# Index scores interleaved pair by pair with the projections of a hybrid attention block on one NeuronCore

## The chip, the core and the metric

One core of one Trainium2 chip runs the whole layer. The metric is device time in microseconds of one execution; the kernel before takes 1416.54 us in the median of three runs (1414.64 to 1420.17). The core's engines run side by side, each through its own queue in order: TensorE (PE, matrix products, with a clock of which a share is granted), VectorE (DVE), ScalarE (ACT), GpSimd (POOL), and SP, which issues the DMAs. Products land in PSUM, from which VectorE and ScalarE read them.

## The reference

A layer with two mixers over the same projected input, then a feed-forward part. What matters here is the first mixer's index scores with their top-k, and the second mixer's decays:

```python
# x: (1, 1024, 1024); h = rms_norm(x); proj = h @ w_in, split into
# q_a, c_kv, q_idx (8 heads of 64), k_idx (64), w_idx (8), q_b, k_b, v_b (4 heads of 128), a_b, b_b, z_b
rel   = relu(einsum('bqhd,bsd->bqhs', qi_b, k_idx))          # per block of 128 rows
score = einsum('bqhs,bqh->bqs', rel, wi_b)
score = where(key_pos < limit, score, -inf)                  # chunk-causal, chunks of 64
_, idx = top_k(score, 256)                                   # the keys that the attention may use
...
g     = cumsum(-exp(a_log) * softplus(a_b + dt_bias))        # in chunks of 64
decay = exp(where(causal, g[..., :, None] - g[..., None, :], -inf))
lower = where(strict, (k * beta) @ k.T * decay, 0);  t_inv = (eye + lower)^-1
...
mix = concat([o_a, o_b]) @ w_out;  x = x + rms_norm(mix)
x = x + rms_norm(square(relu(rms_norm(x) @ w_mlp_in)) @ w_mlp_out)
```

## The kernel before

Products are made in about fp32 precision from split operands: `mm3` (L199 to L201) issues three matmuls, high by high, low by high and high by low. A projection of 128 columns (`project_slowly`) takes eight steps of `mm3` for each half of the 1024 rows, 48 matmuls, into a two-bank accumulator (`psw`, pool of two). The list `plan` gives the order: `kw` (index key, head weights and gates' inputs), four `qi` (two index heads each), four times `kb` and `qb` (a head of k and of q), four `vb`, four `z`, `c`, four `qa`.

What follows a projection depends on its kind. `evac_pair` stores a pair of index heads split into a high and a low part (`QS`, L409 and L410). `conv` (L585 to L590) runs the causal convolution of k, q or v from the accumulator: one ScalarE copy, three VectorE steps over 1024 columns (L587), a ScalarE SiLU. `delta_head` (L679 to L702) turns a head of k and q, sums squares and multiplies the products of k and q with the decays. `base_blocks` (L720 to L722) inverts the small triangles, `post_c` finishes the latents.

`decays(n)` makes the decay matrix of one block of rows: two GpSimd products (L663), two matmuls (L664), an exponential (L666), a select on GpSimd (L667) and a DMA to `e_d`, from which `delta_head` loads. All eight are called behind `kw`. They and the convolutions share a ring of four buffers, `tmp`.

`scores(b)` makes the index scores of one block of 128 queries, chunk by chunk of at most 512 keys: for each of eight heads two matmuls (L480, L481) into one of four banks (`psx`), a ReLU in place on ScalarE (L486), and a multiply-add onto the score in SBUF on VectorE (L487; the first head has one step, L484). All six blocks with a search, 7 down to 2, are called behind the fourth `qi`. Then `pi_close` frees `QS` and `dna` is opened in its place, which holds what `delta_head` needs.

`bisect()` finds the 256th largest score of each row bit by bit, 32 rounds. In a round ScalarE counts three blocks (L521), VectorE three (L527), and VectorE flips the candidate's bit (L530 to L532); the next round needs all of it. Three steps on the least score follow (L548 to L552), and then the masks of the six blocks (L566 to L577). The generator is advanced by the projections: one to three rounds behind each, by the table `rate`, the rest at the end.

`Flow` is a planner that runs while the program is traced. Each part is a generator that yields the time at which it may go on, or the name of an event; the planner takes the first, by rank, that is due, and keeps estimated times of the engines (`use`, with `dve` and `act`). So it fixes the program order, not the executed one: the compiler's scheduler goes through the program in that order as a priority and puts later instructions ahead where an earlier one cannot go. Each engine then executes its queue in order.

When the projections are done, buffers are freed, the event `room` is set, and attention, the delta rule's chain and the output follow.

Of the kernel before, what the change touches and what calls it, by code (L numbers as in the profile page):

```python
# [139 lines left out]
def block_kernel(ctx: ExitStack, tc: tile.TileContext, x, w_in, c_norm, w_uk, w_uv, rel_bias, conv_w, a_log,  # L140
# [148 lines left out]
    warmr = pl.t(px, [P, 1024], F32R, "warmr")  # L289
    V.memset(warmr.bitcast(F32), 0.0)  # L290
    ps = psw()
    for _ in range(10):
        PE.matmul(ps[:, 0:512], warm[:, 0:P], warm, start=True, stop=True)
    ps = psw()
    two = warmr[:, 0:512].rearrange("p (a b) -> p b a", a=2)
    forms = [(warmr[:, 0:P], two), (warmr[:, 0:P], warmr[:, 0:512].rearrange("p (a b) -> p b a", a=4)),
             (warmr[:, 0:256:2], two), (warmr[:, 0:P], warmr[:, 0:256].rearrange("p (a b) -> p b a", a=2))]
    for lhs, rhs in forms:
        o = ps[:, 0:rhs.shape[1] * rhs.shape[2]].rearrange("p (a b) -> p a b", b=rhs.shape[2])
        for _ in range(4):  # L300
            PE.matmul(o, lhs, rhs, start=True, stop=True)
    for _ in range(4):
        for r in range(2):
            rs = slice(64 * r, 64 * r + 64)
            PE.matmul(ps[:, 512 * r:512 * r + 512].rearrange("p (b a) -> p b a", a=2), warmr[rs, 0:P], two[rs],
                      start=True, stop=True)
# [168 lines left out]
    def scores(b):  # L475
        for s0, w in cuts(P * (b + 1)):
            dst = score[:, soff[b] + s0:soff[b] + s0 + w]
            for h in range(8):
                ps = psx()
                PE.matmul(ps[:, :w], QS[:, h, b * P:(b + 1) * P], KH[:, s0:s0 + w], start=True, stop=False)  # L480
                PE.matmul(ps[:, :w], QS[:, h, b * P:(b + 1) * P], KL[:, s0:s0 + w], start=False, stop=True)  # L481
                wh = wab[:, b, h:h + 1]
                if h == 0:
                    V.tensor_scalar(dst, ps[:, :w], 0.0, wh, op0=OP.max, op1=OP.mult)  # L484
                else:
                    S.activation(ps[:, :w], ps[:, :w], AF.Relu)  # L486
                    V.scalar_tensor_tensor(dst, ps[:, :w], wh, dst, op0=OP.mult, op1=OP.add)  # L487
        G.memset(score[0:64, soff[b] + P * b + 64:soff[b] + P * (b + 1)], PAD)
# [461 lines left out]
    def projections():  # L950
        nonlocal dna, dn, dn_close
        for i, (kind, p) in enumerate(plan):
# [19 lines left out]
            if kind == "kw":  # L972
# [3 lines left out]
                for n in range(NB):  # L976
                    decays(n)
# [815 lines left out]
```

## Time and profile before

| | before |
|---|---|
| median of 3 runs | 1416.54 us |
| the profiled execution | 1417.32 us |
| its span, first to last instruction | 1415.6 us |
| mean granted TensorE clock | 0.950 |
| TensorE busy | 1299.8 us, 92% |
| VectorE busy | 1104.6 us, 78% |
| ScalarE busy | 730.1 us, 52% |
| GpSimd busy | 272.0 us, 19% |
| DMA | 211.24 MB, mean 149 GB/s |

Times are from one profiled execution, counted from its first instruction. A share of the span is a mean over stages; the stage that the change touches is the first third, up to about 460 us. "Idle before" is the time that an engine stood ahead of an instruction, and the arrow names what ended it.

### The profile page before, as it was taken

How to read it: one execution, taken by the hardware profiler on the slowest of the kernel's cores; microseconds unless marked ns; L12 is line 12 of the kernel's file. 1: busy time of each engine (PE TensorE's matmuls, PEld its weight loads, DVE VectorE, ACT ScalarE, POOL GpSimd, SP SyncE). 2: the span in 40 equal slices, each digit the busy share in tenths (PEclk: the TensorE clock that was granted, in tenths of full speed). 3: DMA queues.
4: the chain of work that ended last, by engine and by line, in shares of the span. 5: the costliest groups of instructions: out<-in, count | busy, mean ns of one | idle time of the engine just before them, and what ended most of it. 6: DMA issues, size and time to landing. Idle time of an engine off the chain costs nothing. (4 is left out here: it accounts for less than half of the span.)

```text
span 1415.6 us, 20269 instructions
## 1 busy us (share of the span) xinstructions
PE 1299.8 (92%) x6643; PEld 1120.9 (79%) x6643; DVE 1104.6 (78%) x2551; ACT 730.1 (52%) x1521; POOL 272.0 (19%) x296
## 2 busy tenths in 40 slices
PE   7898997998885999999999899999998799999995
PEld 4687894776675899997888688888887688888884
DVE  5524668999999798888768468878876887978975
ACT  5433436777651677677546456566565233333422
POOL 3154221121205335327420000000000000000023
PEclk8899998999995899999999899999999899999998
DMA  6133112456225433333556825555557956645224
GB/s 191 57 85 82 30 46 60 119 157 156 60 72 138 133 95 93 100 116 114 173 163 201 271 101 208 209 208 201 199 200 256 400 173 237 216 141 194 66 79 169
DMA packets 182931, 211.24 MB, mean 149 GB/s; under 512 B 28001, under 2 KB 123434, under 8 KB 182698
## 3 DMA queue, kind: packets, MB, share of 16 engines
q1 hardware_dynamic: 182826, 209.94, 46.3%
q8 instruction: 53, 0.87, 0.3%
q14 instruction: 52, 0.43, 0.1%
HBM read 136.48 MB, written 74.99 MB: 149 GB/s over the span
## 5 line engine op out<-in xcount | busy, mean ns | idle before, releaser
L199 PE MATMUL two<-hTH,wh 128*128 128x512 f32 (+1 forms) x416 | 166.8, 403 | 26.8 <-ACT tmp L424 16.0
L200 PE MATMUL two<-hTL,wh 128*128 128x512 f32 (+1 forms) x416 | 167.0, 401 | 0.0
L201 PE MATMUL two<-hTH,wl 128*128 128x512 f32 (+1 forms) x416 | 165.6, 398 | 0.0
L1750 POOL TENSOR_TENSOR tmp<-acc,c_row 128x512 f32<-128x512 f32 x16 | 20.7, 1302 | 644.3 <-DVE acc L1763 635.3
L199 PEld LDWEIGHTS two<-hTH,wh 128*128 128x128 f32 (+1 forms) x416 | 82.3, 198 | 44.4 <-issue 25.3
L521 ACT ACTIVATE jk<-score,cand 128x1024 bf16<-128x1024 f32 (+2 forms) x96 | 92.5, 966 | 46.0 <-DVE cand L532 29.4
L201 PEld LDWEIGHTS two<-hTH,wl 128*128 128x128 f32 (+1 forms) x416 | 82.1, 197 | 13.0 <-issue 0.8
L200 PEld LDWEIGHTS two<-hTL,wh 128*128 128x128 f32 (+1 forms) x416 | 82.5, 198 | 12.2 <-issue 0.5
L1422 ACT CAST hl<-raw 128x512 fp32r<-128x512 f32 x88 | 52.5, 614 | 53.6 <-PE acc L200 42.8
L1422 ACT CAST hq<-tmp 128x512 fp32r<-128x512 f32 x56 | 34.4, 616 | 79.5 <-PE tr L200 39.0
L270 POOL TENSOR_TENSOR wl<-stg,wh 128x1024 fp32r<-128x1024 f32 (+1 forms) x26 | 60.8, 2341 | 54.1 <-ACT wh L267 52.6
L1423 DVE TENSOR_TENSOR hl<-raw,hl 128x512 fp32r<-128x512 f32 x88 | 59.6, 685 | 7.3 <-ACT hl L1422 7.1
L1158 ACT ACTIVATE big<-big,nm 128x256 f32<-128x256 f32 (+6 forms) x64 | 50.6, 791 | 13.0 <-DVE nm L1157 13.0
L269 POOL TENSOR_SCALAR wh<-stg 128x1024 fp32r<-128x1024 f32 x19 | 19.9, 1048 | 194.0 <-PE two L200 194.0
L1422 ACT CAST hl<-tmp 128x512 fp32r<-128x512 f32 x56 | 33.3, 617 | 44.6 <-DVE tmp L1539 30.3
L1183 ACT CAST part<-tr 128x512 fp32r<-128x512 f32 x80 | 43.2, 543 | 20.3 <-PE tr L1181 16.6
L1184 DVE TENSOR_TENSOR part<-tr,part 128x512 fp32r<-128x512 f32 x80 | 50.2, 630 | 4.4 <-ACT part L1183 4.0
L1206 PE MATMUL acc<-part,VS 128*128 128x256 f32 x288 | 49.4, 295 | 1.3 <-DVE part L1184 1.0
L1422 ACT CAST hl<-tt 128x512 fp32r<-128x512 f32 x56 | 34.5, 615 | 31.1 <-PE tr L200 16.5
L1134 POOL TENSOR_TENSOR mt<-tz,maskb 128x256 f32<-128x256 f32 x56 | 38.5, 692 | 60.2 <-DVE mx L1150 39.6
L199 PE MATMUL sc<-hl,hq 128*128 128x512 f32 x112 | 42.7, 390 | 7.4 <-ACT hq L1422 7.4
L587 DVE SCALAR_TENSOR_TENSOR tmp<-two,svT,tmp 128x1023 f32<-128x1023 f32 (+2 forms) x36 | 45.5, 1275 | 4.0 <-ACT tmp L585 2.9
(514 smaller groups left out, 4161.5 us busy)
## 6 DMA issues: line engine op xcount, KB each, us to landing
hid<-tmp SPq DMA_DIRECT2D x140, 256.0 KB, 2.3
hq<-hid SPq DMA_DIRECT2D x80, 256.0 KB, 4.8
raw<-in_w_mlp_in_dram SPq DMA_DIRECT2D x14, 1024.0 KB, 5.6
raw<-in_w_mlp_out_dram SPq DMA_DIRECT2D x14, 1024.0 KB, 6.8
tmp<-hid SPq DMA_DIRECT2D x56, 256.0 KB, 5.2
stg<-in_w_in_dram SPq DMA_DIRECT2D x25, 512.0 KB, 4.2
x<-in_x_dram SPq DMA_DIRECT2D x8, 512.0 KB, 5.4
la_d<-la SPq DMA_DIRECT2D x8, 512.0 KB, 3.7
```

The lines of the kernel that those rows point to most:

```text
L199: PE.matmul(o, lh, rh, start=start, stop=False, skip_group_check=more)
L200: PE.matmul(o, lh, rl, start=False, stop=False, skip_group_check=more)
L201: PE.matmul(o, ll, rh, start=False, stop=stop, skip_group_check=more)
L270: G.tensor_sub(wl[:, :, :n], f[:, :, :n], wh[:, :, :n].bitcast(F32))
L521: S.activation(junk[:, :n], s_of(b), AF.Sign, bias=cand[:, 3 + i:4 + i].bitcast(F32), scale=-1.0, accum_out=cnt[:, 3 + i:4 + i])
L587: V.scalar_tensor_tensor(acc[:, 3 - j:T], both[:, 0:T - 3 + j], w[j], acc[:, 3 - j:T], op0=OP.mult, op1=OP.add)
L1158: S.activation(pr[:, :n], pr[:, :n], AF.Exp, bias=nm, accum_out=den[:, hh:hh + 1])
L1183: S.copy(pt[:, 0:2 * nj, 0, :], v4(ps)[:, 0:2 * nj])
L1184: V.tensor_sub(pt[:, 0:2 * nj, 1, :], v4(ps)[:, 0:2 * nj], pt[:, 0:2 * nj, 0, :].bitcast(F32))
L1206: PE.matmul(po[:, hh * 256:hh * 256 + 256], VS[:, j + a, 2 * p + hh, :], pt[:, 2 * a + hh].rearrange("p a t -> p (a t)"), start=j + a + hh ...
L1422: S.copy(h_, src)
L1423: eng.tensor_sub(l_, src, h_.bitcast(F32))
```

## The change

The scores become a generator of their own, which goes through the pairs of heads and, for each, through all blocks; the search, too, is a stream of the planner, with estimated times. The decays are called behind the first `kb` and the first `qb`, four each. Memory of the queries is freed in the first `qb`. Of the warm-up products at the start, 24 of other forms on a zeroed tile `warmr` are replaced by 24 more of the first form. The heart of the diff:

```diff
-    for _ in range(10):
+    for _ in range(34):
         PE.matmul(ps[:, 0:512], warm[:, 0:P], warm, start=True, stop=True)
...
-    def scores(b):
-        for s0, w in cuts(P * (b + 1)):
-            dst = score[:, soff[b] + s0:soff[b] + s0 + w]
-            for h in range(8):
-                ps = psx()
...
+    def scoring():
+        for p in range(4):
+            yield ("qi", p)
+            for b in range(NB - 1, 1, -1):
+                for s0, w in cuts(P * (b + 1)):
+                    dst = score[:, soff[b] + s0:soff[b] + s0 + w]
+                    for h in (2 * p, 2 * p + 1):
+                        while flow.bank("px", 4) > flow.now:
+                            yield flow.bank("px", 4)
+                        ps = psx()
+                        PE.matmul(ps[:, :w], QS[:, h, b * P:(b + 1) * P], KH[:, s0:s0 + w], start=True, stop=False)
+                        PE.matmul(ps[:, :w], QS[:, h, b * P:(b + 1) * P], KL[:, s0:s0 + w], start=False, stop=True)
+                        wh = wab[:, b, h:h + 1]
+                        t = flow.pe(2 * w / 2260)
+                        if h == 0:
+                            V.tensor_scalar(dst, ps[:, :w], 0.0, wh, op0=OP.max, op1=OP.mult)
+                        else:
+                            S.activation(ps[:, :w], ps[:, :w], AF.Relu)
+                            V.scalar_tensor_tensor(dst, ps[:, :w], wh, dst, op0=OP.mult, op1=OP.add)
+                            t = act(t, w / 1200 + 0.18)
+                        flow.took("px", dve(t, w / 960 + 0.16))
+                        yield 0.0
+        for b in range(NB - 1, 1, -1):
+            G.memset(score[0:64, soff[b] + P * b + 64:soff[b] + P * (b + 1)], PAD)
+        flow.done("scored", flow.rings["px"][-1])
...
     def bisect():
+        yield "scored"
...
+            ta = td = flow.now
             for i, b in enumerate(ACB):
+                ta = act(ta, n / 1200 + 0.45)
...
             for i, b in enumerate(DVB):
+                td = dve(td, n / 960 + 0.28)
...
-            yield
+            yield dve(max(ta, td), 0.8)
...
-            yield
+            yield dve(flow.now, 3 * n / 960 + 0.6)
...
-            yield
+            yield dve(act(flow.now, n / 1200 + 0.4), 5.5 * n / 960 + 1.0)
+        flow.done("topk", flow.now)
...
-    topk = bisect()
-    rate = {"kb": 1, "qb": 1, "vb": 2, "z": 3, "c": 3, "qa": 3}
...
             if kind == "kw":
                 post_kw()
                 gates()
                 bias()
-                for n in range(NB):
-                    decays(n)
-            elif (kind, p) == ("qi", 3):
-                for b in range(NB - 1, 1, -1):
-                    scores(b)
-                pi_close()
-                dna, dna_close = pl.open("dna", side="right")
+            elif kind == "qi":
+                flow.done(("qi", p), dve(act(flow.now, 1.2), 1.4))
...
                 if kind == "vb":
                     conv(loaded["both"], blk, v_d[:, :, p, :])
+                    act(dve(act(flow.now, 1.05), 3.7), 1.1)
                 else:
+                    act(dve(act(flow.now, 1.05), 3.7), 1.1)
+                    if p == 0:
+                        for n in range(4 * (kind == "qb"), 4 + 4 * (kind == "qb")):
+                            decays(n)
+                    if kind == "qb" and p == 0:
+                        yield "scored"
+                        pi_close()
+                        dna, dna_close = pl.open("dna", side="right")
...
                     if kind == "qb":
                         delta_head(p, kqh)
+                        dve(act(flow.pe(5.2), 4.0), 9.5)
...
-                        flow.done("base", flow.now + BASE)
+                        flow.done("base", dve(flow.now + 3.0, 30.0) + 8.0)
...
-            for _ in range(rate.get(kind, 0)):
-                next(topk, None)
-        for _ in topk:
-            pass
+        yield "topk"
         flow.done("projections", flow.now)
...
-    for rank, gen in enumerate((chain(), levels(0), levels(1), emits(), projections())):
+    for rank, gen in enumerate((chain(), levels(0), levels(1), emits(), scoring(), bisect(), projections())):
         flow.add(rank, gen)
```

The later streams get ranks that are two higher, in the same order.

## Rows read from the trace of the kernel before

**Rows 1.** The page's engine totals: busy us, share of the span, instructions.
```profile
PE 1299.8 (92%) x6643; PEld 1120.9 (79%) x6643; DVE 1104.6 (78%) x2551; ACT 730.1 (52%) x1521; POOL 272.0 (19%) x296
```

**Rows 2.** Stretches: us PE, PEld, DVE, ACT, POOL busy; PE clock; DMA share; GB/s.
```profile
57.00:70.00 13.00, 12.73 (x61) 9.74 (x59) 7.94 (x17) 5.69 (x9) 4.73 (x2) 1.00 0.43 138
57.00:114.00 57.00, 56.67 (x266) 48.11 (x265) 18.32 (x36) 20.27 (x33) 33.42 (x28) 1.00 0.36 102
114.00:230.00 116.00, 109.08 (x494) 90.84 (x492) 74.22 (x102) 50.14 (x90) 29.98 (x26) 0.97 0.19 50
230.00:459.00 229.00, 185.26 (x833) 155.86 (x832) 220.82 (x563) 137.59 (x285) 55.70 (x36) 0.88 0.41 113
421.00:459.00 38.00, 21.30 (x100) 18.01 (x100) 37.27 (x49) 9.59 (x20) 19.76 (x12) 0.62 0.59 139
```

**Rows 3.** VectorE's timeline: start us, us, line, operation; idle before it and releaser.
```profile
69.22 0.69 DVE L410 SCALAR_TENSOR_TENSOR QS<-two,QS 64x512 fp32r<-64x512 f32 x1
...
229.40 0.62 DVE L487 SCALAR_TENSOR_TENSOR score<-ch,wab,score 128x384 f32<-128x384 f32 x1
...
457.72 0.94 DVE L577 TENSOR_SCALAR maskb<-jk 128x384 bf16<-128x384 bf16 x1
```

**Rows 4.** TensorE's timeline in the scoring stretch.
```profile
113.77 0.40 PE L480 MATMUL tr<-KH,QS 128*128 128x512 f32 x1
...
130.18 0.77 PE L199 MATMUL two<-hTH,wh 128*128 128x512 f32 x1 [1.74 <-DVE tmp L587]
...
138.04 0.38 PE L201 MATMUL two<-hTH,wl 128*128 128x512 f32 x1
138.25 0.38 PE L199 MATMUL two<-hTH,wh 128*128 128x512 f32 x1
138.47 0.39 PE L480 MATMUL ch<-KH,QS 128*128 128x512 f32 x1
```

**Rows 5.** VectorE's timeline, the compares that end a search round.
```profile
256.86 1.54 DVE L531 TENSOR_TENSOR t<-cnt,lim 128x6 int32<-128x6 f32 x1
...
347.79 0.17 DVE L531 TENSOR_TENSOR t<-cnt,lim 128x6 int32<-128x6 f32 x1 [0.47 <-ACT jk L521]
...
351.26 0.17 DVE L531 TENSOR_TENSOR t<-cnt,lim 128x6 int32<-128x6 f32 x1 [0.47 <-ACT jk L521]
```

**Rows 6.** VectorE's groups by line from 60 to 470: count, busy us, mean ns, idle.
```profile
L587 DVE SCALAR_TENSOR_TENSOR tmp<-two,svT,tmp 128x1023 f32<-128x1023 f32 (+2 forms) x36 | 45.5, 1275 | 4.0 <-ACT tmp L585 2.9 <-POOL wh L269 0.9
...
L527 DVE TENSOR_SCALAR_CACHE_REDUCE pre<-score,cand 128x896 bf16<-128x896 f32 (+2 forms) x48 | 39.8, 829 | 0.3
L487 DVE SCALAR_TENSOR_TENSOR score<-ch,wab,score 128x512 f32<-128x512 f32 (+3 forms) x40 | 26.0, 655 | 24.9 <-ACT ch L486 23.6
...
L530 DVE TENSOR_SCALAR bare<-cand 128x6 int32<-128x6 int32 x31 | 10.8, 347 | 0.0
...
L531 DVE TENSOR_TENSOR t<-cnt,lim 128x6 int32<-128x6 f32 x31 | 8.8, 284 | 2.2 <-ACT jk L521 1.6
```

**Rows 7.** GpSimd's groups by line from 57 to 459, those of the decays.
```profile
L663 POOL TENSOR_TENSOR tmp<-upto,gp 128x512 fp32r<-128x512 f32 x16 | 16.3, 1042 | 7.2 <-ACT gp L648 4.7 <-DMA e_d<-tmp 2.4
...
L667 POOL TENSOR_SCALAR_AFFINE_SELECT tmp<-tmp 128x512 f32<-128x512 f32 x8 | 5.1, 638 | 8.7 <-ACT tmp L666 8.7
```

**Rows 8.** GpSimd's timeline, the subtraction beside a slow compare.
```profile
256.01 2.38 POOL L270 TENSOR_TENSOR wl<-stg,wh 128x1024 fp32r<-128x1024 f32 x1
```

**Rows 9.** TensorE's timeline at the start.
```profile
1.26 4.45 PE L293 MATMUL two<-warm 128*128 128x512 bf16 x10 [1.26 <-DVE warm L288]
...
15.51 2.68 PE L337 MATMUL tr<-ident,x 128*128 128x128 f32 x8 [4.76 <-DVE x L333]
18.75 0.72 PE L199 MATMUL two<-hTH,wh 128*80 128x512 f32 x1 [0.56 <-ACT hTH L339]
```

**Rows 10.** ScalarE's timeline, the last store of h.
```profile
46.05 0.69 ACT L339 ACTIVATE hTH<-tr,svT 128x512 fp32r<-128x512 f32 x1 [0.29 <-PE tr L337]
```

More of the change, by code (lines that the diff above doesn't have):

```diff
@@ L288, in block_kernel @@
     V.memset(warm, 0.0)
-    warmr = pl.t(px, [P, 1024], F32R, "warmr")
-    V.memset(warmr.bitcast(F32), 0.0)
     ps = psw()
-    for _ in range(10):
+    for _ in range(34):
         PE.matmul(ps[:, 0:512], warm[:, 0:P], warm, start=True, stop=True)
[L294 to L306, printed above, removed]
     xs = []
@@ L473, in bias @@
         SY.dma_start(tz_d, src)
-    def scores(b):
-        for s0, w in cuts(P * (b + 1)):
-            dst = score[:, soff[b] + s0:soff[b] + s0 + w]
-            for h in range(8):
-                ps = psx()
[L480 to L488, printed above, removed]
+    def scoring():
[23 more added lines that the diff above has]
+        flow.done("scored", flow.rings["px"][-1])
     DVB, ACB = [6, 3, 2], [7, 5, 4]
@@ L737, in block_kernel @@
     flow = Flow()
-    BASE = 90.0
     T4, M4 = 0.44, 0.88
@@ L1392, in block_kernel @@
     for rank, gen in enumerate((setup(), tails(), sums(), logits(), turns(), weights(), add_rows_of_x(), turn_h2(), out_proj())):
-        flow.add(rank + 5, gen)
+        flow.add(rank + 7, gen)
     flow.run("attention")
```

## The prediction

> **What bounds the kernel now.** I read the page's engine totals first: TensorE (PE) is busy 92% of the span, VectorE (DVE) 78% [rows 1]. A mean over unlike stages decides nothing, so the next view is the table of stretches, cut at the events that the change touches [rows 2]. From 57 to 114 us TensorE projects the index queries and VectorE is busy for only 18.3 us of 57. From 114 to 230 the scores are made beside the first projections of k and q: TensorE 109 of 116 us, VectorE 74. From 230 to 459 it is the other way round: VectorE 220.8 of 229 us (96.4%), TensorE 185, and its granted clock falls to 0.88 in the mean. In the last 38 us of it TensorE has 21 us of work at a mean clock of 0.62 and VectorE is full. So the whole first part, up to 459, is worth two sums: VectorE has 18.3 + 74.2 + 220.8 = 313.4 us of work in 402 us, TensorE less than 351 (some of it at the low clock). Neither needs 402. The loss is an order in which first the one and then the other is short of work.
>
> Where that comes from shows in the timelines. The first two query heads are stored at 69.9 [rows 3], yet the first score matmul starts at 113.77 [rows 4]; all scores stand in program order behind the fourth pair of heads. And the end of the part is set by VectorE: the last mask row ends at 458.7 [rows 3]. The search behind the scores is a chain of 32 rounds, each at best 3.47 us long (compare at 347.79 to compare at 351.26), of which VectorE stands idle for 0.47 us in one wait for ScalarE's last count, and in slivers beside it [rows 5].
>
> **Part 1: scores pair by pair.** No score work is removed or added. It is 80 pieces (ten chunks of columns by eight heads), two matmuls each, and on VectorE 80 x 0.655 = 52.4 us (one row of the three stands in [rows 6]; the other two have the same mean). They may now start at about 70 instead of 113.8. TensorE's share: matmuls of 512 columns stand 0.216 us apart at full clock (starts 138.04 and 138.25 [rows 4]); the chunks of one head have 4224 columns, so eight heads and two matmuls are 67,584 columns, 28.5 us. A projection is 48 such matmuls, 10.4 us. After 57 there are 3.5 index projections left (one half ran earlier): 36 us. So TensorE could finish the scores at 57 + 36 + 28.5 + about 2 for small products = 124, plus 10.4 for each k or q projection that slips in between. At least two will (there are two accumulators that fill without VectorE): 145. At the other end stands the pace of before: 116 us for the scoring stretch [rows 2], less some 8 us in which TensorE stood or ran at the lower clock in it (116 - 109 by [rows 2], and a little for the first matmuls after such a wait, 0.77 us long instead of 0.38 [rows 4]), from 70 on: 178. What sets the pace there is the executed order, in which projection matmuls stand between the pieces although the scores come first in the program; the same compiler pass orders the new program, so I take 170, nearer to the old pace. TensorE then has room for four k and q projections by that time.
>
> VectorE by 170: 7.9 us done from 57 to 70 [rows 2], 12 more stores of queries at 0.69 [rows 3], 8.3; about 3 for the gates; scores 50 (the 52.4 less overlapping ends); three or four convolutions at 3 x 1.275 [rows 6], 15. Sum 84. Left: 313.4 - 84 = 229 us.
>
> **Part 2: search rounds by an estimate.** Before, one to three rounds are traced behind each projection; now a round is traced when the estimated ScalarE and VectorE times allow it, and the projections' generator waits for the masks at its end. The work is the same. The rounds can run from 170 on instead of 230, when the last piece of a score was added [rows 3]. Their counts on VectorE (48 at 0.83 us in the one half of the rounds [rows 6], as many in the other) and all VectorE work behind them now begin some 60 us earlier, which is where the gain is. The wait for "scored" stands in front of the second half of q's first step: behind it on the generator are the delta heads, and they needed the scores' memory before too. Behind the wait for the masks stands only the event that frees buffers for the attention, which came last before as well. How full can VectorE be? 96.4% as before with convolutions beside the rounds; about 80% where a round runs alone (0.47 and the slivers of 3.47 [rows 5]). I take 94%: eight convolutions, the heads and the base blocks are left to lie beside the rounds.
>
> **Part 3: the decays.** They lay beside the index projections, free. Now four of them stand behind the k and four behind the q projection. Each costs two matmuls (16 of 512 columns in all, 4 us, within TensorE's slack), an exponential, two products and a select on GpSimd: 16.3 + 5.1 = 21.4 us in all [rows 7], a 256 KB store on SP's queue with nothing late behind it, and two buffers of the ring of four that the convolutions use. The GpSimd work is the price: in VectorE's full stretch it gets in the way. A compare of six columns that takes 0.17 us elsewhere took 1.54 us from 256.86 on and ended at 258.40, as a GpSimd subtraction (256.01, 2.38 us) ended [rows 5, 8]. Bounds: nothing, if all of it falls beside the scores (where VectorE's operands come from PSUM), and 21.4 if each microsecond blocks one. Over the old stretch, the flips (31 x (0.347 - 0.17)) and compares (31 x (0.284 - 0.17)) [rows 6] lost 9 us against 55.7 us of GpSimd work [rows 2], a sixth: I take 4 us. A gain is excluded, as none of the work is left out.
>
> The Trainium skill's page "SBUF — State Buffer" (section "Who interferes with whom") speaks against this move: VectorE and GpSimd share one pair of ports, held for a whole instruction, and the second to ask blocks. The compare above agrees with it, 1.54 against 0.17 us. Taken without mercy, the rule puts the upper bound, 21.4, in the place of the 4 us, and the time would be some 18 us longer.
>
> **Part 4: the warm-up.** 24 matmuls of other forms are replaced by 24 more of the first. The old ones and a small transpose ended at 10.75, and the next product waited 4.76 us for x, until 15.51 [rows 9]. The new ones end at 5.7 + 24 x 0.216 = 10.9. Nothing. If all took the first ten's 0.445 us each [rows 9], they would end at 16.4, 0.9 us late.
>
> **The sum.** VectorE's rest at 170 is 229 + 4 = 233 us; at 94% that is 248, and the part ends at 418 instead of 459, 41 us earlier. TensorE must fit: 17 projections (177 us), the heads' products (128 of them, some 30) and the decays (4) are 211 us in 248; it fits, with 37 us to spare. Behind 459 nothing is changed but the planner's clock readings, which may shift the attention's interleaving by a few us either way. The profiled execution took 1417.3 us (span 1415.6), 0.8 over the median of 1416.5; 1417.3 - 41 = 1376.
>
> **Rivals.** (a) Better packing: the scores finish at 145, with 69 us of VectorE done and no loss to GpSimd: 244 / 0.964 = 253, end at 398, gain 61: 1356; a little more if convolutions slip in, 1352. For it: queues run as fast as the chip lets them, and VectorE has 42 us of holes from 114 to 230. (b) Less packing: scores at 178, the whole 21.4 us blocked: (313.4 - 84 + 21.4) / 0.94 = 267, end at 445, gain 14: 1403. (c) The change does not do what it says: tracing order is only a wish, and the executed order already mixes score and projection matmuls [rows 4]. If the queries' later stores had to wait for earlier pairs' score matmuls, all would stand as before: 1417. Against it: the first projection reads of h began while later parts of h were still being written (18.75, against a store at 46.05 [rows 9, 10]), so order is kept by region, not by tile. (d) Slower: the search takes VectorE before the convolutions do. Then both accumulators stay full, and TensorE stands still for the rounds, 32 x 3.47 = 111 us; it still has 211 us to do: 170 + 111 + 211 = 492, 33 us later, 1450. It decides from the point where TensorE's idle time between the scores' end and 459 exceeds 459 - 170 - 211 = 78 us; before, it stood 44 us of the 229 [rows 2]. The rank of the new streams, ahead of the projections, speaks for it; that a round cannot use VectorE without a pause, and that each later convolution then slips in, speaks against it.
>
> **How the numbers follow.** Forecast, 1363 to 1391: 0.50. (a) 0.15. (b) 0.18. (c) 0.08. (d) 0.09. About 0.5%, 7 us, is what a measurement of this kernel can tell from no change; (a), (b) and the forecast lie beyond it: faster 0.83, same 0.08, slower 0.09. The range takes in (a) and most of (b): 1352 to 1408.
>
> **What would show it.** Right: score matmuls from about 70 between index projections; the first search round ending near 175 rather than behind 230; VectorE above 90% from then on; the last mask row near 418; everything behind shifted as a block. Part 3 is wrong if small VectorE operations between 170 and 300 are not longer than before. The forecast falls if the last scores come after 200, or if TensorE waits for accumulators by more than 78 us.

## The result and the profile after

The changed kernel takes 1431.49 us in the median of four runs (1428.17 to 1438.07) against 1415.59 us for the kernel before on the same chip: a ratio of 1.011, interval 1.0085 to 1.0136. It is slower by 16 us where 41 us less was forecast. The profiled execution took 1429.22 us, its span is 1427.5 us. In the code of after the score matmuls are L471 and L472, ScalarE's ReLU L478, VectorE's adds L476 (first head) and L479, the decays L665 to L670, the convolution's VectorE step L589, the rounds L521 to L533, the masks L567 to L578, and the stores of the last projections L409 (before: L424).

The page's engine totals of after, as in [rows 1]:

```profile
PE 1300.1 (91%) x6643; PEld 1114.0 (78%) x6643; DVE 1115.7 (78%) x2550; ACT 731.5 (51%) x1523; POOL 266.1 (19%) x296
```

TensorE has the same work, 1300.1 us against 1299.8, and the span is 11.9 us longer: TensorE is idle for 1427.5 - 1300.1 = 127.4 us instead of 1415.6 - 1299.8 = 115.8. The stretches of after, with the columns of [rows 2] and its bounds, and two more around the place of the loss:

```profile
57.00:114.00 57.00, 53.82 (x242) 43.59 (x241) 35.88 (x64) 25.12 (x45) 11.58 (x6) 0.97 0.22 65
114.00:230.00 116.00, 91.47 (x372) 70.07 (x372) 89.11 (x190) 80.75 (x156) 38.76 (x41) 0.85 0.20 55
160.00:200.00 40.00, 23.00 (x70) 14.88 (x70) 32.88 (x76) 32.40 (x59) 23.72 (x29) 0.73 0.19 52
200.00:220.00 20.00, 13.26 (x55) 11.35 (x56) 17.95 (x40) 15.23 (x30) 0.00 (x0) 0.69 0.28 80
230.00:459.00 229.00, 202.65 (x956) 172.79 (x955) 190.63 (x446) 101.62 (x205) 60.98 (x41) 0.96 0.43 117
421.00:459.00 38.00, 33.74 (x191) 28.97 (x189) 6.09 (x19) 5.96 (x17) 14.78 (x13) 1.00 0.67 178
```

VectorE did what was hoped: 17.6 us more than before from 57 to 114, 14.9 more from 114 to 230. TensorE lost 17.6 us from 114 to 230 (91.47 against 109.08), all of it from 160 to 220, where its granted clock is about 0.7, and from 421 on it is TensorE that is busy (33.74 of 38 us) and VectorE that stands (busy for 6.09, before 37.27).

VectorE's timeline of after (columns as in [rows 3]): the end of the first search round, the last mask, the last base block.

```profile
173.61 0.17 DVE L533 SCALAR_TENSOR_TENSOR cand<-t,bare 128x6 int32<-128x6 int32 x1
...
405.63 0.25 DVE L578 TENSOR_SCALAR maskb<-jk 128x384 bf16<-128x384 bf16 x1
...
420.87 1.09 DVE L724 COPY kqh<-kqh 128x1024 f32<-128x1024 f32 x1
```

TensorE's timeline of after: the first score, decays that hold the first convolutions up, the longest wait, and the matmul at which full speed is back.

```profile
70.14 0.50 PE L471 MATMUL ch<-KH,QS 128*128 128x512 f32 x1 [0.24 <-DVE QS L395]
...
160.43 0.34 PE L471 MATMUL ch<-KH,QS 128*128 128x384 f32 x1
...
175.33 0.80 PE L666 MATMUL ch<-tmp,after_r 128*128 128x512 f32 x1 [2.52 <-POOL tmp L665]
176.33 0.80 PE L666 MATMUL ch<-tmp,after_r 128*128 128x512 f32 x1 [0.20 <-POOL tmp L665]
178.85 0.80 PE L666 MATMUL tr<-tmp,after_r 128*128 128x512 f32 x1 [1.73 <-POOL tmp L665]
180.34 0.77 PE L199 MATMUL two<-hTH,wh 128*128 128x512 f32 x1 [0.69 <-DVE tmp L589]
...
206.74 0.77 PE L199 MATMUL two<-hTH,wh 128*128 128x512 f32 x1 [10.03 <-DVE tmp L589]
...
211.99 0.49 PE L199 MATMUL two<-hTH,wh 128*128 128x512 f32 x1
```

Scores start at 70.14 (forecast: about 70), end at 163 (170), the first round ends at 173.8 (near 175), the last mask at 406 (near 418), and VectorE's long work is over at 422; from 170 to 422 it is busy for 239.0 of 252 us, 95%. What the forecast named of the scores, the search and VectorE came, and the time did not. The stretches of the projections alone (accumulators `two`; columns as in [rows 2] without GpSimd's) tell where it went. The first x in a line counts matmuls, 48 to a projection. Of the kernel before:

```profile
57.00:170.00 113.00, 94.56 (x396) 76.02 (x394) 26.76 (x29) 13.85 (x20) 0.97 0.29 80
170.00:230.00 60.00, 39.76 (x161) 29.27 (x159) 7.65 (x6) 2.23 (x2) 1.00 0.16 44
230.00:480.00 250.00, 153.75 (x624) 124.74 (x624) 22.76 (x18) 16.99 (x24) 0.86 0.43 118
```

And of after:

```profile
57.00:170.00 113.00, 64.45 (x268) 50.54 (x266) 11.61 (x17) 9.22 (x16) 0.96 0.18 52
170.00:230.00 60.00, 35.38 (x129) 27.79 (x130) 12.53 (x11) 4.34 (x4) 0.76 0.25 70
230.00:480.00 250.00, 184.37 (x784) 150.86 (x783) 33.14 (x26) 19.30 (x26) 0.96 0.45 124
```

By 170, 102 score matmuls more than before are done (all 160 instead of 58) and 128 projection matmuls fewer, mostly an exchange. But from 170 to 230, with no scores left, TensorE gets through 2.7 projections only, fewer than the 3.4 that it made beside scores before. At 230 it has 16.3 to do, not 13. The last store (L409) starts at 455.28 (before 433.1). The last transposed copy of the latents (tile `CT`, L1098, before L1097), which I take as the end of the part, starts at 464 (before 459).

### The profile page after: what moved, and what is told of

Same layout as the page of the kernel before. It is cut to its first block, busy times and chain, and to the rows that moved or that the text cites. A ratio compares the mean times of both kernels' runs of the same rounds, so it can differ in the third digit from the quotient of the medians.

```text
span 1427.5 us, 20247 instructions
## 1 busy us (share of the span) xinstructions
PE 1300.1 (91%) x6643; PEld 1114.0 (78%) x6643; DVE 1115.7 (78%) x2550; ACT 731.5 (51%) x1523; POOL 266.1 (19%) x296
## 5 line engine op out<-in xcount | busy, mean ns | idle before, releaser
L199 PE MATMUL two<-hTH,wh 128*128 128x512 f32 (+1 forms) x416 | 167.5, 405 | 33.7 <-ACT tmp L409 15.6
L521 ACT ACTIVATE jk<-score,cand 128x1024 bf16<-128x1024 f32 (+2 forms) x96 | 92.3, 965 | 24.4 <-DVE cand L533 20.8
L1182 PE MATMUL tr<-ident,big 128*128 128x128 f32 x288 | 46.1, 274 | 0.9 <-DVE part L1185 0.7
```

What stands on the lines that cost most here:

```text
L199: PE.matmul(o, lh, rh, start=start, stop=False, skip_group_check=more)
L521: S.activation(junk[:, :n], s_of(b), AF.Sign, bias=cand[:, 3 + i:4 + i].bitcast(F32), scale=-1.0, accum_out=cnt[:, 3 + i:4 + i])
L1182: PE.transpose(ps[:, c * P:(c + 1) * P], u["p"][hh][:, (j + a) * P:(j + a + 1) * P], ident)
```

## The experiments

The theory after the result: buffers of a pool are handed out in program order, so a step that is called later in the program stands behind all earlier users of its buffers, and ahead of all later ones. The decays use the scores' PSUM banks (`psx`) and the convolutions' ring `tmp`. Behind `kb` they come after the last score in the one and before the first convolution in the other, and TensorE, its two accumulators full, waits for convolutions. The rivals: pair order costs by itself; the search as a stream takes VectorE; GpSimd blocks VectorE; or the end is set by ScalarE's stores.

All runs, in the order of the text. "Scores" goes from the first score matmul to the start of VectorE's last add, "first convolution" is its first VectorE step, "part" is the end of the part as above. Each ratio is to the kernel before on the same chip in the same series; as that kernel's own median lies between 1413.8 and 1418.0 us in the series, ratios are compared, and medians only within a series (the first letter of a name).

| run | what it is | median, us | ratio to before [interval] | scores, us | first convolution | part, us |
|---|---|---|---|---|---|---|
| before | | 1415.59 | 1 | 114-229 | 123 | 459 |
| after | all three parts | 1431.49 | 1.0110 [1.0085, 1.0136] | 70-163 | 176 | 464 |
| e1_decays_back | after, decays behind `kw` | 1425.41 | 1.0063 [1.0040, 1.0086] | 115-230 | 125 | 470 |
| e2_decays_moved | before, decays moved alone | 1434.30 | 1.0132 [1.0094, 1.0169] | 75-170 | 182 | 472 |
| e3_scores_only | before, pair order alone | 1420.25 | 1.0029 [1.0008, 1.0050] | 114-228 | 124 | 470 |
| e4_search_only | before, search stream alone | 1410.45 | 0.9963 [0.9941, 0.9985] | 114-230 | 124 | 463 |
| f5_no_psum | before, decays' matmuls left out | 1396.95 (one) | - | 75-215 | 111 | 439 |
| f1_own_tiles | after, decays not in `tmp` | 1421.71 | 1.0039 [1.0014, 1.0064] | 68-190 | 129 | 460 |
| f2_block_own | e2, decays not in `tmp` | 1425.82 | 1.0077 [1.0052, 1.0103] | 76-215 | 112 | 472 |
| f7_search_moved_own | e4, decays moved and not in `tmp` | 1436.75 | 1.0157 [1.0123, 1.0190] | 75-214 | 110 | 486 |
| g2_acc_block | before, decays in the accumulators | 1430.32 | 1.0094 [1.0074, 1.0114] | 68-237 | 138 | 460 |
| g3_acc_search | g2, search stream | 1422.69 | 1.0030 [1.0012, 1.0048] | 67-236 | 137 | 472 |
| g4_acc_after | after, decays in the accumulators | 1424.21 | 1.0045 [1.0029, 1.0062] | 70-182 | 149 | 453 |
| g5_acc_scores | g4, rounds by the table | 1413.11 | 0.9976 [0.9956, 0.9996] | 71-183 | 150 | 454 |
| h1_after_signs | after, sign counts ahead | 1436.23 | 1.0142 [1.0112, 1.0172] | 69-162 | 175 | 467 |
| h2_acc_signs | g5, sign counts ahead | 1408.03 | 0.9931 [0.9903, 0.9958] | 70-182 | 149 | 451 |
| h3_search_signs | e4, sign counts ahead | 1417.71 | 1.0018 [0.9993, 1.0042] | 112-228 | 121 | 463 |
| h5_vector_search | e4, decays on VectorE | 1403.17 | 0.9914 [0.9882, 0.9947] | 108-220 | 118 | 452 |
| j2_three_after | after, decays between the pairs | 1414.76 | 1.0016 [0.9993, 1.0039] | 69-186 | 158 | 440 |
| j9_three_scores_v | j2 on VectorE, rounds by the table | 1415.17 | 1.0015 [0.9995, 1.0034] | 70-193 | 165 | 455 |

**The parts one by one (e1 to e4).** Of e1 against after, and of e2 against before, the edit is the same move:

```diff
-                for n in range(NB):        # behind kw
-                    decays(n)
+                    if p == 0:             # behind the first kb and the first qb
+                        for n in range(4 * (kind == "qb"), 4 + 4 * (kind == "qb")):
+                            decays(n)
```

> The changed kernel with one part undone: all eight decays called behind kw again. Theory D (the decays, traced behind the scores, wait for PSUM banks until the scores are done at 160 us and hold the first convolutions, and with them both accumulators, until 176 to 215): the first convolution step starts before 135, TensorE's hole from 160 to 215 closes, the last projection is stored some 30 us earlier than 455, total 1385 to 1400. Theory S (the search stream takes VectorE and ScalarE ahead of the convolutions and the projections' stores, whatever the decays do): the hole stays, with the rounds running in it, total 1420 to 1432. Theory P (scores in pairs are at fault by themselves): also 1420 or more, with the scores done at 160 as now.

> The kernel before with one part of the change alone: four decays behind the first k, four behind the first q projection. Theory D: the decays wait behind the block of scores, the first convolution moves from 123 to behind the scores (past 200), both accumulators stay full and TensorE stands: 1435 to 1460. Theories S and P: the decays are free beside other work: 1412 to 1422.

> Scores pair by pair alone: decays behind kw, search rounds by the old table (the round of the first k projection goes with the first q). Theory D: scores done near 160, convolutions from before 135, total 1385 to 1405. Theory P: 1420 or more. Theory S: faster than before, 1380 to 1405, and faster than the run with the decays moved back and the search stream kept.

> The search as a stream with estimated times alone: scores in one block behind the fourth pair, decays behind kw. Theory S: rounds run ahead of convolutions and stores, the last projection is stored later than 433, total 1425 to 1440. Theory D: no change beyond 7 us, 1410 to 1422. Theory P: the same, 1410 to 1422.

The move alone costs 1.3%, 18 us, as much as the whole change (the intervals overlap). Pair order alone costs 0.3%, the search as a stream alone gains 0.4%. The parts do not simply add: pair order and stream together (e1) stand at 1.0063, where the two alone multiply to 0.9992, and in their company the move costs only the difference of 1.0110 and 1.0063. And the scores' start follows the decays, not the order of the scores: with pairs and the decays behind `kw` (e1) the first score runs at 115.14, with blocks behind the fourth pair and the decays moved (e2) at 74.62. The stretches of e2 show the loss of after in the same place, TensorE 86.08 of 116:

```profile
57.00:114.00 57.00, 56.66 (x265) 48.75 (x265) 25.66 (x46) 20.25 (x35) 18.43 (x10) 1.00 0.27 77
114.00:230.00 116.00, 86.08 (x317) 57.32 (x316) 95.54 (x188) 82.03 (x160) 31.12 (x37) 0.85 0.16 45
230.00:472.00 242.00, 214.30 (x997) 182.57 (x995) 201.15 (x468) 107.04 (x215) 64.96 (x42) 0.94 0.42 114
```

By its total e2 stands next to the theory's range and far from the rivals', and e4 met the theory. But e1 and e3 missed the theory's 1385 to 1405 and met the rivals' 1420 or more. They do not price pair order, though, as their scores still start at 114 or later, and the trace shows another cause. Their last stores (429 and 427) and last masks (451 and 449) come earlier than before (433 and 458). Yet the part ends at 470: TensorE stands 22.91 us before a product of the delta rule's chain, which waits for GpSimd, and the second half of the latents' transposes (L429, also in a tile `ch`) stands behind it in TensorE's queue. In the kernel before both halves run by 388. TensorE's timeline of e1:

```profile
387.98 0.60 PE L429 MATMUL tr<-ident,tmp 128*128 128x128 f32 x4
...
450.15 1.97 PE L794 MATMUL ch<-te,lo 128*128 128x64 f32 x8 [22.91 <-POOL te L780]
...
458.78 1.06 PE L429 MATMUL ch<-ident,tmp 128*128 128x128 f32 x4
```

In e3 it is the same wait (22.91, until 448.37); in after the second half runs at 452.98, 42 us behind the first. No run moves it, so what it costs in the total is open.

**Which ring (f5, f1, f2).** f5 takes the decays out of the PSUM banks and leaves the rest of them where it was; f1 and f2 take them out of `tmp`:

```diff
-        ps = psx()                                                            # f5
-            PE.matmul(ps, after_r, gm..., start=i == 0, stop=i == 1)
-        S.activation(e, v4(ps), AF.Exp)
+        S.activation(e, gms[:, 0].bitcast(F32), AF.Exp)
...
-        gms = pl.t(ph, [P, 2, 4, P], F32R, "tmp", bufs=4)                     # f1, f2
+            gm = pl.t(ph, [P, 4, P], F32R, "jk", bufs=2)
-        e = tmp4()[:, 0:512]...
+        e = pl.t(ph, [P, 4, P], F32, "pre")
```

> The kernel before with the decays' two matmuls left out (the exponential reads the products themselves, so the decays' values and what follows from them are other ones); everything else stands where it stood, the scores behind the fourth pair in program order. Theory R: without the decays in the PSUM rings the first score matmul moves from 113.8 to about 75. If the scores start late because they are traced behind the fourth pair: 105 or later.

> The changed kernel, but the decays' products and exponentials lie in tiles that the search uses later, not in the ring of four of the convolutions. Theory R (rings of buffers are handed out in program order: the scores' PSUM banks put the decays behind the scores, and the ring of four puts the convolutions behind the decays): convolutions start before 125 while the scores still run, the scores end later than 163, TensorE's hole from 160 to 215 is gone; total 1395 to 1415. Theory S (the search stream, not the ring, keeps the convolutions and the projections waiting): the hole stays and the total is 1420 or more.

> The kernel before with the decays moved behind the first k and q projections, and in tiles of their own; scores in a block, rounds by the table. Theory R: scores from about 75 and convolutions from about 85, the 18 us that moving the decays alone cost are gone, 1395 to 1415. If what that move cost was not the ring but GpSimd work beside VectorE: 1430 or more.

f5 settles the start. TensorE's timeline of f5, the first score; before it stood at 113.77 [rows 4]:

```profile
75.45 0.40 PE L480 MATMUL tr<-KH,QS 128*128 128x512 f32 x1
75.68 0.39 PE L481 MATMUL tr<-KL,QS 128*128 128x512 f32 x1
```

Nothing else was moved, and the scores, in blocks behind the fourth pair, start 38 us earlier. (f5's total is of one run with less work and other values, and is not compared.) In the kernel before, the matmul of a decay runs in the same tile `tr` just ahead of the first score:

```profile
113.54 0.40 PE L664 MATMUL tr<-tmp,after_r 128*128 128x512 f32 x1
```

f1 settles the second ring: out of `tmp`, the decays no longer stand ahead of the convolutions, which start at 129 beside the scores, and TensorE's hole is gone. The stretches of f1:

```profile
114.00:230.00 116.00, 116.00 (x551) 102.07 (x550) 71.22 (x95) 49.71 (x84) 53.37 (x50) 1.00 0.23 64
230.00:459.00 229.00, 172.31 (x771) 146.17 (x771) 205.27 (x540) 134.40 (x277) 54.49 (x38) 0.84 0.44 118
```

It ends at 460 nonetheless, and its total missed the theory's 1395 to 1415: the decays are still behind the scores' banks, now from 190 to 237, the heads wait for them (first products at 252, in after at 238), and VectorE has its hole later. f2 has f1's hole too, and missed the same range: between 200 and 275 VectorE waits 16.7 us for the heads' ScalarE step, and 6.9 us for the decays' stores from `pre`, a tile that the search uses too. f7, the same move on the search stream's version, stands at 1.0157 where e4 stood at 0.9963.

**Other buffers for the decays (g2, g4, g5).** Two decays behind each pair of heads' projection, in the projections' accumulators:

```diff
-        ps = psx()
+                pair = psw()               # behind each qi
+                for i in range(2):
+                    decays(2 * p + i, pair[:, 512 * i:512 * i + 512])
```

> The kernel before with one difference: the decays' products land in the projections' two-bank accumulators, two decays behind each pair of index heads, instead of in the scores' banks. Scores in a block, rounds by the table. Theory R: as in the run without the decays' matmuls, scores from about 75, first convolution before 110, last mask row near 440, total 1395 to 1405. If the run without the decays' matmuls was faster for another reason (less work on TensorE, or a single lucky time): 1412 or more.

> The changed kernel with one difference: decays in the projections' accumulators, two behind each pair of index heads, as early as scores. Theory R: the convolutions are no longer behind them, scores done near 155, VectorE full from there, as the prediction reckoned: part ends near 425, total 1380 to 1400. If the prediction's sum was wrong for another reason as well (the end set by TensorE's late projections whatever the decays do): 1410 or more, with the last projection stored past 445.

> As the run before this one with the search rounds by the old table. Theory R: the pair order now shows its worth, scores done near 155 instead of 212 with the block: faster than the block by up to 15 us, 1380 to 1400. If the order of the scores is worth nothing even then: as the block, 1395 to 1405.

In g4 the scores start at 70 and the decays are done at 126, and VectorE's last mask ends at 428, yet the last projection is stored at 448. Here the projections and the decays share a ring: in g2 TensorE waits there for the decays' exponentials (3.7 us) and for stores of queries, and from 57 to 110 it is busy for 41.0 of 53 us, in g4 for 46.5. The ring that the decays leave is paid by the ring that they enter. Against after, g4 is lower by 0.6%, and g5, with the rounds by the table, by 1.3%. None of the three came to the theory's totals (1395 to 1405, and 1380 to 1400); g2 and g4 met the other expectation, g4 with its words that TensorE's late projections set the end whatever the decays do.

The stream of the search has no fixed price. With scores in a block it gains 0.4% (e4 against before) and 0.5% to 0.6% (g3 against g2, 1422.69 and 1430.32), or costs 0.8% (f7 against f2). With scores pair by pair it costs in both cases where little else differs: 0.3% from e3 to e1, where the intervals touch, and 0.7% from g5 to g4, where they do not. So a part of what after lost can be the stream's.

**ScalarE's queue (h1 to h3).** TensorE waits 15.6 us in after for the stores L409, which stand in ScalarE's queue behind sign counts that wait for masks. In the kernel before it is 16.0 us. The counts are issued together, ahead of the masks:

```diff
+        for i, b in enumerate(DVB + ACB):
+            S.activation(j1[:, :n], s_of(b), AF.Sign, bias=thr[:, i:i + 1], ..., accum_out=sgs[:, i:i + 1])
         for b in range(NB - 1, 1, -1):
-            S.activation(j1[:, :n], sb, AF.Sign, bias=th, scale=-1.0, accum_out=sg)
```

> The changed kernel with the six sign counts of the masks issued together, ahead of the first mask, into one tile; nothing else is moved. In the changed kernel each count waits on ScalarE for the mask before it (maskb 16.8 us, need 7.6 us) and the projections' stores stand behind it in ScalarE's queue, so TensorE waits 15.6 us for them between 377 and 401. Theory (the queue of ScalarE passes VectorE's chain on to the last projections): these waits fall to under 5 us, the last store of a projection comes at 440 to 446 instead of 455 and the total falls by 8 to 15 us, to 1417 to 1424. Rival (TensorE has only its own backlog from the hole at 160 to 215, and the waits are only moved): the last store stays at 450 to 456 and the total within 4 us of 1431.

> The version with scores pair by pair, rounds by the table and decays two by two in the projections' accumulators (1413 us, VectorE done at 429, last store at 450, part's end at 454), with the sign counts issued together ahead of the masks. Theory of ScalarE's queue: TensorE's wait for the stores falls from 18.5 us to under 6, the last store comes at 436 to 442 and the part ends at 440 to 446, total 1398 to 1406. Rival (TensorE's own work of the last projections sets the end): part's end 450 to 455, total 1409 to 1415.

> The search as a stream alone (1410 us, masks end at 457, VectorE busy to the end), with the sign counts issued together. Both theories: here VectorE's masks end last, so the counts' waits (16.5 us) cost nothing by themselves. Theory of ScalarE's queue: the masks themselves no longer wait for counts that stand behind stores, a gain of 0 to 4 us; 1406 to 1411. Rival: no change, 1409 to 1413, and the last store still near 429.

This theory fell. TensorE's waits in h1 from 230 to 465 (what waited, for what, us in total, times, the longest):

```profile
PE ch L796 <- POOL te L782: 15.1, 1, 15.1
PE two L199 <- ACT tmp L409: 8.0, 4, 3.8
```

The wait for stores is halved, but a single wait of 15.1 us, for GpSimd in the chain of the delta rule, has come up; the last store starts at 462 (in after 455), and the part ends at 467. In h2 the total is lower by half a per cent than in g5, but the wait for stores is still 14.5 us, so its gain is not the one that was expected; its cause stays open. h3 is 0.5% slower than e4, which neither expectation had.

**The decays' pace (h5).** The two products and the masking of each decay on VectorE, which has room until 230:

```diff
-            G.tensor_tensor(gm, upto..., b4(gp[:, i, n, :]), OP.mult)
+            V.tensor_tensor(gm, upto..., b4(gp[:, i, n, :]), OP.mult)
-        G.affine_select(e, e, ..., fill=0.0, base=0, channel_multiplier=-1)
+        V.tensor_tensor(e, e, upto[:, None, :].to_broadcast(H4), OP.mult)
```

> The search as a stream alone, with the decays' 16 products and 8 masks on VectorE instead of GpSimd (the masking as a product with the triangle). Theory (the scores' first buffers are held by the decays that are allocated ahead of them, so their start follows the decays' pace): with two fewer crossings to GpSimd for each of eight, the decays pass in 30 to 38 us instead of 45, the scores start at 100 to 108 instead of 114 and end as much earlier, the part ends 5 to 10 us earlier, 1400 to 1407. Rival (the pace is TensorE's queue and ScalarE's exponential, and VectorE's evictions of the qi projections stand in the way): scores still from 112 to 116, and 1410 to 1416.

The total is as the theory had it, and its ratio is the lowest of all complete kernels (h2's interval overlaps it); the pace is for the most part the rival's. TensorE's timeline of h5, the decays' matmuls (L669):

```profile
74.20 0.39 PE L669 MATMUL tr<-tmp,after_r 128*128 128x512 f32 x1
74.43 0.38 PE L201 MATMUL two<-hTH,wl 128*128 128x512 f32 x1
74.65 0.39 PE L669 MATMUL tr<-tmp,after_r 128*128 128x512 f32 x1
...
79.84 0.40 PE L669 MATMUL ch<-tmp,after_r 128*128 128x512 f32 x1
...
85.48 0.40 PE L669 MATMUL tr<-tmp,after_r 128*128 128x512 f32 x1
```

The first decays still pass 5.64 us apart, with 24 projection matmuls between, half a projection; in e4, with GpSimd, three of the first five gaps are 5.65 us too (the others 6.08 and 6.50). Only the last come sooner: the seventh stands 5.66 us behind the sixth, in e4 8.45 (108.30 against 113.71). The scores start 5 us earlier and end 10 earlier, and the part ends at 452 instead of 463.

**The decays between the pairs (j2, j9).** The last test of the theory leaves pairs, stream and buffers of after as they are and moves only the calls:

```diff
+            for n in range(*((0, 3), (3, 6), (6, 8), (8, 8))[p]):     # behind pair p's scores
+                decays(n)
...
-                    if p == 0:
-                        for n in range(4 * (kind == "qb"), 4 + 4 * (kind == "qb")):
-                            decays(n)
```

> The changed kernel with the decays neither behind all scores nor ahead of them: three behind the first pair of heads' scores, three behind the second and two behind the third, in the shared buffers as before. Their place in the two rings is then ahead of the last pair's scores and of every convolution. Theory (the cost of the change is the decays' place in the rings: behind the last scores and ahead of the first convolution): scores from 70, decays done by 150, the convolutions start at 140 to 155 beside the last scores instead of at 176, TensorE's busy time in 160 to 220 rises from 36 to over 50, the last projection is stored by 440 instead of 455 and the part ends at 440 to 452; total 1405 to 1418. Rival (scores pair by pair cost by themselves, wherever the decays are, since TensorE's projections fall back behind them): last store still at 450 or later, total 1421 to 1431.

> The same places for the decays, their products and masks on VectorE instead of GpSimd, and the search rounds by the table. Theory of the place in the rings: as in the version before, scores from 70 to about 170, convolutions from about 145, with decays that pass some 5 us sooner as VectorE makes their products; the part ends at 438 to 450, total 1398 to 1412. Rival (pairs cost by themselves): no better than with the decays in the accumulators, 1411 to 1420.

The stretches of j2:

```profile
57.00:114.00 57.00, 54.18 (x245) 44.58 (x245) 32.81 (x60) 24.45 (x44) 19.45 (x15) 0.97 0.26 75
114.00:230.00 116.00, 107.18 (x488) 87.99 (x486) 85.80 (x169) 67.94 (x131) 37.86 (x36) 0.96 0.26 73
230.00:440.00 210.00, 182.53 (x852) 154.06 (x850) 198.42 (x475) 114.14 (x233) 59.59 (x37) 0.95 0.42 114
```

TensorE has 107.18 of 116 us again, VectorE keeps its lead, and the part ends at 440, 24 us earlier than in after and 19 earlier than in the kernel before. The ratio falls from 1.0110 to 1.0016 [0.9993, 1.0039], as the theory had it: the place of the decays was most of the loss, and with it mended pair order and stream together cost nothing that can be told. But the 19 us are not in the total either. Cut at the end of the part and where the last tail of the attention has passed, the profiled spans are 459 + 276 + 681 before and 440 + 284 + 688 in j2. In the second piece TensorE is idle for 15.8 us instead of 9.1, as the attention's first exponential starts only 13 us earlier; in the third it has 647.2 us of work instead of 639.9, 31 matmuls that had been done earlier before. So of the 19 us 8 are given back in the one and 7 in the other, which leaves 4 in these two executions and, by the ratio, nothing; by what stream was not tried. j9, with the products on VectorE and the rounds by the table, stores the last projection at 450 and gains nothing: convolutions at 165, part at 455, 1415 us, which is the rival's forecast and not the theory's. As it differs from j2 in two things, which of them lost the 15 us at the part's end is open, and j2 with the table alone was not tried.

## Why the prediction was wrong

**What bounds the kernel.** Right: VectorE's work moved forward brings its end forward, to 422. Wrong: the cause of the late first score. The text took program order behind the fourth pair of heads; f5, e1 and e2 show that the decays ahead of the scores in the shared banks held them. The rows to see it stood in the trace, the decays' matmuls from 76 to 121 and the first score at 113.77 in the same tiles `tr` and `ch`. So the move of the decays, priced as a cost only, is what gave the early scores.

**Part 1** was right in its times (70 and 163), but TensorE had two k and q projections done by 170 where room for four was counted.

**Part 2** was right in its times: the first round at 173.8, the search over at 406, VectorE 95% busy where 94% was taken. That the stream costs nothing beside pair order is not borne out (g4 against g5).

**Part 3** is the step that failed. Its price, 4 us of GpSimd in VectorE's way, did not occur. By the text's own test, the flips and compares take 404 and 215 ns in the mean against 347 and 284 [rows 6], 19.2 us against 19.6. Single ones are held as told: a flip took 2.02 us at 197.35 while a GpSimd subtraction ran from 197.00 to 199.34. But there are few, and the sums show that they decided nothing here. The Trainium skill's page "SBUF — State Buffer" (section "Who interferes with whom") gives the rule for such a pair, that the second to ask waits for the port; the 2.02 us agree with it. What did cost was named in the prediction beside that price, and priced at nothing: the "two buffers of the ring of four that the convolutions use". In after, no convolution starts before all 70 of VectorE's adds are done, at 163; before, six convolutions stood among the adds. The decays' matmuls wait for GpSimd at 175.33 to 178.85 and take 0.80 us each instead of 0.40, and behind the last decay (193) a projection has 10.03 us to wait for its convolution. The term measured 18 us where the move stands alone (e2). In after, calling the decays between the pairs instead (j2) ends the part 24 us earlier and takes 0.9%, some 13 us, off the total. The flips and compares of after, with the columns and the window of [rows 6]:

```profile
L531 DVE TENSOR_SCALAR bare<-cand 128x6 int32<-128x6 int32 x31 | 12.5, 404 | 0.0
L532 DVE TENSOR_TENSOR t<-cnt,lim 128x6 int32<-128x6 f32 x31 | 6.7, 215 | 7.1 <-ACT jk L521 6.5
```

**Part 4** was right: the first product starts at 18.71, before at 18.75 [rows 9].

**The sum** failed at "it fits, with 37 us to spare". From 170 to 464 TensorE had 246.2 us of work, not 211: 19 projections instead of 17, and at a lower clock (0.92 in the mean), 219.75 us for them, 11.6 each instead of 10.4. All its other matmuls took 26.5 us, within the 34 counted. To that come 47.8 us of idle time, 28.8 of it for accumulators: 246.2 + 47.8 = 294, and 170 + 294 = 464. The text looked for an idle time of more than 78 us before it would doubt; 48 were enough, as the 37 to spare were not there. So rival (d), both accumulators full and TensorE late, came true in kind, with the convolutions held by the decays instead of by the search, and with 5 us at the part's end instead of 33. The decays are not the whole of it: in j2, without their hole, TensorE from 170 to 440 still has 240.2 us of work (18.8 projections, 11.5 us each) and 29.8 of idle time, 270 in place of the 248 forecast. So of the 46 us by which the part's end was missed, 24 are the decays' place, and 22 stay in a kernel that has them well placed. The stretches behind these sums, first of after, then of j2 (columns as in [rows 2]):

```profile
170.00:464.00 294.00, 246.24 (x1126) 208.05 (x1127) 247.28 (x576) 154.39 (x303) 82.65 (x60) 0.92 0.40 110
...
170.00:440.00 270.00, 240.17 (x1134) 204.09 (x1133) 248.48 (x588) 150.59 (x304) 75.13 (x52) 0.96 0.40 109
```

And of the projections alone, after and j2:

```profile
170.00:464.00 294.00, 219.75 (x912) 178.65 (x912) 45.68 (x36) 23.64 (x30) 0.92 0.40 110
...
170.00:440.00 270.00, 215.92 (x904) 174.60 (x903) 38.28 (x30) 21.35 (x28) 0.96 0.40 109
```

**The rest of the program** was taken to shift as a block. It did not: in the profiled executions the 5 us at 464 become 12 at the end of after, and the 19 us gained in j2 become 4. No complete kernel came near the 41 us; the lowest ratio is h5's 0.9914, 12 us.

## What to carry to other kernels

A step that is moved in the program moves in every pool it draws from: list its buffers, and for each the users that it now follows and those that it now precedes, and ask what of them was ahead of whom in the trace. A forecast that frees one engine has to count the other engine's work that is left at that point, from the trace, by pieces (here projections of 48 matmuls), and its idle time over the whole program, since the end of one stage is not the end of the kernel. Where a step's start is explained by program order, look first which tile it writes, and who had that tile last.

## What the runs showed of the hardware

TensorE's granted clock fell to 0.73 from 160 to 200 and 0.69 from 200 to 220, when it was busy for 36.3 of 60 us, and was 1.00 in that stretch before at 59.8 of 60; a matmul of 512 columns that came after a wait there took 0.77 to 0.80 us instead of 0.38 to 0.40, twice as long, which is the lower of the two levels, 1.2 instead of 2.4 GHz. Behind the wait of 10.03 us, twelve matmuls took from 206.74 to 211.99, 5.25 us, where twelve at the 0.216 us of the prediction take 2.6. So a hole on TensorE was paid twice here: by its length, and by the slow matmuls behind it.
